# Attention scores of the second block on half-array tiles, and trailing means on VectorE

## The chip, the core and the metric

The kernel runs on one core of one Trainium2 chip. The metric is the device time of one execution in microseconds, as a median of several runs. A core has five engines that run in parallel, each with its own instruction queue: TensorE (PE in the profile), VectorE (DVE), ScalarE (ACT), GpSimd (POOL) and SyncE (SP), which here issues nearly all DMA transfers in the order of its queue.

## What is computed

The reference runs two transformer blocks over 256 tokens of width 1024. The first block (two layers: a linear-recurrent mixer and an attention, each with a feed-forward part) is not touched. In the second block the input is projected, and three things are computed side by side: a convolution with a layer norm, a sparse attention, and trailing means. They are joined, multiplied with an output matrix, added to the input, and a mixture of experts follows. What the change touches, cut:

```python
# sparse attention, a block of 128 queries at a time
rel = relu(einsum('bqhd,bsd->bqhs', qi_block, ki))        # indexer: 8 heads of 64, one key of 64
score = einsum('bqhs,bqh->bqs', rel, wi) * idx_scale      # then the 64 best keys of each query
q = einsum('btc,chd->bthd', cq, w_uq)                     # 8 heads of 64
# scores of the softmax over the chosen keys alone, then probabilities times values

# trailing means over windows of 2, 4, 8, 16 tokens, one for each of four groups of 64 channels
cs = cumsum(u); mean = (cs - cs shifted by w) / min(n_pos, w)
out = (mean - u) @ pool_w[g] * pool_scale
```

## The kernel before

All tensors stay on chip as float32; activations are held as features x tokens (128 partitions, 256 tokens), so a head of 64 features takes half of the 128 partitions, and two heads share a tile. Large products are made of three products of a high and a low part: `split_tile` (L115 loads, L122 rounds on ScalarE, L123 subtracts on VectorE, or on GpSimd when `eng` says so), `mm3` (L143 to L145).

The function `second` (L1171 on) is the second block up to the output product. It is written in program order; a planner orders each engine's instructions by that order as priority and by its own estimate of when inputs are ready, so that late steps fill gaps. `tc.issue_after` holds steps behind a named one. In program order:

- `proj(c0, use)` loads 256 columns of the input weights, splits them (on VectorE; for c0 = 1536 on GpSimd) and multiplies; `use` takes the result out of PSUM. Order: 1024 and 1280 (convolution), 0 (latent key, and `kib`, the indexer's key), 256 and 512 (the indexer's queries `qi`), 768 (query latent), 1536 (`pe`, the input of the trailing means).
- `index(j2)`, L1271, twice: for two pairs of heads j and two blocks b of queries one matmul over all 128 rows (L1277). Both heads' queries are the weights, and `kib` holds the key twice, block-diagonally, with zeros elsewhere (L1252, L1253 set them on GpSimd), so that head 0 and head 1 fall into different columns of the result. A Relu on ScalarE (L1279) and weighted sums on VectorE (L1283, L1285) follow.
- `kbd[j]`: the keys of a head pair, block-diagonal in the same way: two memsets on GpSimd (L1315, L1316), a matmul (L1318), two copies of 64 partitions on ScalarE (L1319, L1320). Then the values (L1323).
- eight rounds of top-8 on VectorE (L1332, L1334), and the mask (L1336).
- `soft(j)`, L1366, for four head pairs: scores (L1373), masked maximum on VectorE (L1377, L1378), exponentials on ScalarE (L1380), normalisation (L1382, L1385, L1387). `context(j, e)`, L1390: transposes (L1395), copies (L211, L213), values (L1400, L1401), split.
- `pool_mean`, L1408: eight steps on GpSimd (L1411 to L1418) behind two memsets; `pooled` multiplies (L1423).
- `convolved`, L1426: 46 steps on VectorE (L1434, L1436) and a layer norm with transposes (L1444, L1459); last in program order, so it fills gaps.
- `out2`, L272: the output product in four slabs of weights, of which the second half of the second slab is split on GpSimd; first slab from contexts 0 and 1, second from 2 and 3, third from the trailing means, fourth from the convolution.

The order at the end is written out: soft(0); then for j = 0 to 3: soft(j+1), context(j), the trailing means after j = 0, `pooled` after j = 1, the convolution after j = 3.

The expert weights of the mixture (196 pieces of up to 1 MB) are loaded by `fetch` (L1512, L1514) into buffers in turn: ten that are free early, then five in the pool `we`, which takes the place in memory of the second block's pools R2 and following (`kbd` was allocated first there, then `qi`, `sel`, `c2`, ... the convolution's `cv`), then buffers of the output weights and of the splits.

Of the kernel before, what the change touches and what calls it, by code (L numbers as in the profile page):

```python
# [9 lines left out]
F32 = mybir.dt.float32  # L10
# [9 lines left out]
S = 256  # L20
# [32 lines left out]
def tile_body(ctx, tc, a, out, stop=None, dbg=None):  # L53
# [17 lines left out]
    def psb():  # L71
        return ppool[0].tile([128, 512], F32, name="pb")
# [1098 lines left out]
    def second(R, diag, mcf, yT, raw, turned, last_square, ss2, consts):  # L1171
# [6 lines left out]
        def t2(name, slot):  # L1178
            return R2.tile([128, 2, 16 + S], F32, name=name, tag=f"t{slot}")
# [8 lines left out]
        nc.sync.dma_start(kvg, a["kv_g"].partition_broadcast(128))  # L1188
        kbd = [R2.tile([128, 2, S], F32, name=f"kbd{j}") for j in range(4)]
        qi = R2.tile([128, 4, S], F32, name="qi", tag="q")  # L1190
# [40 lines left out]
        def proj(c0, use, eng=None):  # L1231
            w = split_cols(a["w_z"][:, c0:c0 + 256], 256, eng)
            for i in range(2):
                p = psa()[:, 0:256]
                mm_feat3(p, w[i], hT, KT)
                use(i, p)
# [12 lines left out]

        kib = t2("kib", 1)[:, :, 0:S]  # L1250
        with tc.issue_after(after.ins):
            G.memset(kib[64:128, 0, :], 0.0)  # L1252
            G.memset(kib[0:64, 1, :], 0.0)  # L1253

        def use0(i, p):
            if i == 0:
                A.copy(ck, p)
            else:
                V.tensor_copy(kib[0:64, 0, :], p[0:64, :])
                A.copy(kib[64:128, 1, :], p[0:64, :])  # L1260
                A.activation(wf8[64:72, :], p[64:72, :], AF.Copy, scale=512.0 ** -0.5)
# [9 lines left out]
        def index(j2):  # L1271
            for j in (2 * j2, 2 * j2 + 1):
                for b in range(2):
                    nk, sc = 128 * (b + 1), sel[b]
                    p = psb()
                    p2 = p[:, 0:2 * nk].rearrange("p (h k) -> p h k", h=2)
                    T.matmul(p2, qi[:, j, b * 128:(b + 1) * 128], kib[:, :, 0:nk], start=True, stop=True)  # L1277
                    rel = RD.tile([128, 2, 256], F32, name="rel", tag="de", padded_shape=[128, 2, 384])
                    A.activation(rel[:, :, 0:nk], p2, AF.Relu)  # L1279
                    for i in range(2):  # L1280
                        w = wit[:, b, 2 * j + i:2 * j + i + 1]
                        if j + i == 0:
                            V.tensor_scalar(sc, rel[:, i, 0:nk], w, None, op0=mult)  # L1283
                        else:
                            V.scalar_tensor_tensor(sc, rel[:, i, 0:nk], w, sc, op0=mult, op1=add)  # L1285
        p = psb()
# [25 lines left out]
        for j in range(4):  # L1312
            t = kbd[j]
            with tc.issue_after(after.ins):
                G.memset(t[64:128, 0, :], 0.0)  # L1315
                G.memset(t[0:64, 1, :], 0.0)  # L1316
            p = psb()
            T.matmul(p[:, 0:256], w_uk[:, j * 128:(j + 1) * 128], ckT, start=True, stop=True)  # L1318
            A.copy(t[0:64, 0, :], p[0:64, 0:256])  # L1319
            A.copy(t[64:128, 1, :], p[64:128, 0:256])  # L1320
        for b in range(2):
# [40 lines left out]
        G.memset(pe[:, :, 0:16], 0.0)  # L1362
        proj(1536, lambda i, p: A.copy(pe[:, i, 16:], p), G)
        prefetch()

        def soft(j):  # L1366
            e = RD.tile([128, 2, 384], F32, name="de", tag="de")
            for b in range(2):
                nk = 128 * (b + 1)
                o = 0 if b == 0 else 128  # L1370
                p = psa()
                p2 = p[:, 0:2 * nk].rearrange("p (h k) -> p h k", h=2)
                T.matmul(p2, qT[:, j, b * 128:(b + 1) * 128], kbd[j][:, :, 0:nk], start=True, stop=True)  # L1373
                st = RW.tile([128, 8], F32, name="dst", bufs=4)
                eb = e[:, :, o:o + nk]
                for i in range(2):
                    V.tensor_tensor_reduce(eb[:, i, :], p2[:, i, :], sel[b], 1.0, -3e38, add, amax, st[:, i:i + 1])  # L1377
                V.tensor_scalar(st[:, 2:4], st[:, 0:2], rq[:, b:b + 1], -1.0, op0=mult, op1=mult)  # L1378
# [29 lines left out]
        def pool_mean():  # L1408
            G.memset(s2[:, :, 0:16], 0.0)
            G.memset(s4[:, :, 0:16], 0.0)  # L1410
            G.tensor_tensor(s2[:, :, 1:], pe[:, :, 1:], pe[:, :, 0:15 + S], add)  # L1411
            G.tensor_tensor(s4[:, :, 2:], s2[:, :, 2:], s2[:, :, 0:14 + S], add)
            G.tensor_tensor(s2[:, 1, 4:], s4[:, 1, 4:], s4[:, 1, 0:12 + S], add)
            G.tensor_copy(s2[64:128, 0, :], s4[64:128, 0, :])
            G.tensor_copy(s4[64:128, 1, :], s2[64:128, 1, :])
            G.tensor_tensor(s2[64:128, 1, 8:], s4[64:128, 1, 8:], s4[64:128, 1, 0:8 + S], add)
            G.tensor_tensor(pm, pm, pinv, mult)
            G.tensor_tensor(pm, pm, pe[:, :, 16:], sub)  # L1418

# [611 lines left out]
```

## Time and profile before

| | |
|---|---|
| median of 3 runs | 1334.0 us |
| the runs | 1334.43, 1330.85, 1334.0 us |
| profiled execution | 1335.32 us, span 1333.5 us |
| busy in the span: PE, DVE, ACT, POOL | 1166.8, 729.2, 491.3, 249.9 us |
| mean granted clock of TensorE | 0.936 |
| moved by DMA | 361.82 MB |

The span runs from the first to the last instruction of the profiled execution. Busy time is summed over all stages; what bounds one stage is read from tables by stretch and from timelines. A float32 matmul of the program appears as two records. A record "64*64" has 64 rows and 64 columns of the array. "idle" and the arrow behind a row say how long the engine had waited before it and which instruction ended the wait.

### The profile page before, as it was taken

The page shows a single profiled execution, that of the slowest core. Times are in us where ns is not written, and L with a number is a line of the kernel's source. Part 1 is how long each engine was busy: PE and PEld are TensorE (multiplying, and loading weights), DVE is VectorE, ACT ScalarE, POOL GpSimd, SP SyncE. Part 2 cuts the span into 40 slices and gives each one's busy share as a digit, 9 for nine tenths or more (in the row PEclk, how much of TensorE's full clock was granted, in tenths as well). Part 3 has the DMA queues.
Part 4 walks back from the last instruction along what each step waited for, and adds up shares of the span by engine and source line. Part 5 has one row for each costly group of instructions (what it writes and reads, how often), then busy time and mean ns, then how long its engine had stood idle before and what let it go on. Part 6 is the DMA issues. An engine that isn't in the chain of part 4 may idle for free.

```text
span 1333.5 us, 18894 instructions
## 1 busy us (share of the span) xinstructions
PE 1166.8 (87%) x7392; PEld 853.4 (64%) x7392; DVE 729.2 (55%) x1297; ACT 491.3 (37%) x857; POOL 249.9 (19%) x259
## 2 busy tenths in 40 slices
PE   7988899999999999999999999998877776666764
PEld 7987798988988888898999888662322131212211
DVE  6869947677687887657664789851112010101102
ACT  5624426454444656546444555620000000000002
POOL 5533330321211351122222233300000000000000
PEclk8999899999999999999999999999987677978788
DMA  7432206767775553667775853699999999999996
GB/s 243 132 90 92 80 33 218 264 237 284 279 289 190 173 186 127 219 234 248 255 243 179 332 193 138 245 357 420 418 420 418 420 417 419 420 417 421 418 421 262
DMA packets 129214, 361.82 MB, mean 271 GB/s; under 512 B 13408, under 2 KB 69344, under 8 KB 105568
## 3 DMA queue, kind: packets, MB, share of 16 engines
q1 hardware_dynamic: 126560, 359.24, 71.8%
q10 hardware_dynamic: 2560, 1.31, 0.4%
q8 instruction: 60, 0.98, 0.3%
q14 instruction: 34, 0.28, 0.1%
HBM read 358.96 MB, written 1.57 MB: 270 GB/s over the span
## 4 chain that ended last, share of the span: by engine, by line
PE 53%; DMA 28%; DVE 11%; issue 3%; ACT 3%; POOL 1%; SPq 0%; DVEq 0%; ACTq 0%; POOLq 0%
DMA ew<-in_exp_w_dram 15%; PE acc L144 9%; PE acc L143 9%; PE acc L145 9%; DMA ew<-in_exp_w2b_dram 8%; DMA wm<-in_mod_w_dram 4%; PE pb L143 3%; PE pb L145 3%; PE pb L144 3%; DVE s L123 3%; PE pb L1730 2%; PE pb L1704 2%; PE pb L1696 1%; PE pf L1704 1%; PE acc L1735 1%
## 5 line engine op out<-in xcount | busy, mean ns | idle before, releaser
L123 DVE TENSOR_TENSOR s<-w,s 128x1024 fp32r<-128x1024 f32 x224 | 285.2, 1276 | 93.1 <-ACT s L122 93.0
L122 ACT CAST s<-w 128x1024 fp32r<-128x1024 f32 x240 | 250.9, 1046 | 117.1 <-PE acc L145 88.7
L144 PE MATMUL pb<-xTh,s 128*128 128x256 f32 x512 | 144.3, 282 | 0.8 <-DVE s L123 0.8
L143 PE MATMUL pb<-xTh,s 128*128 128x256 f32 x512 | 144.5, 282 | 0.6 <-ACT xTh L153 0.6
L145 PE MATMUL pb<-xTl,s 128*128 128x256 f32 x512 | 144.1, 281 | 0.0
L942 POOL TENSOR_TENSOR ul<-u,uh 128x256 fp32r<-128x256 f32 x64 | 86.8, 1356 | 252.7 <-ACT uh L941 252.7
L144 PE MATMUL acc<-s,ul 128*128 128x512 f32 x256 | 100.5, 393 | 0.7 <-POOL ul L942 0.6
L143 PE MATMUL acc<-s,uh 128*128 128x512 f32 x256 | 100.1, 391 | 0.0
L145 PE MATMUL acc<-s,uh 128*128 128x512 f32 x256 | 99.7, 390 | 0.0
L143 PEld LDWEIGHTS pb<-xTh,s 128*128 128x128 f32 x512 | 96.1, 188 | 4.7 <-issue 1.7
L144 PEld LDWEIGHTS pb<-xTh,s 128*128 128x128 f32 x512 | 96.2, 188 | 4.0 <-DVE s L123 2.0
L145 PEld LDWEIGHTS pb<-xTl,s 128*128 128x128 f32 x512 | 98.0, 191 | 0.4 <-DVE xTl L154 0.4
L1709 DVE SCALAR_TENSOR_TENSOR big<-big,pb 128x512 f32<-128x512 f32 x8 | 5.5, 687 | 164.1 <-ACT big L1708 164.1
L143 PE MATMUL acc<-xTh,s 128*128 128x256 f32 x320 | 93.2, 293 | 2.2 <-ACT xTh L1225 1.5
L1704 PE MATMUL pb<-ew,big 128*32 128x512 f32 x448 | 68.8, 710 | 28.1 <-DMA ew<-in_exp_w_dram 24.0
L1730 PE MATMUL pb<-ew,big 128*32 128x512 f32 (+1 forms) x544 | 75.6, 672 | 19.8 <-DMA ew<-in_exp_w2b_dram 14.2
L1704 PE MATMUL pf<-ew,big 128*32 128x512 f32 x448 | 69.1, 724 | 27.3 <-DMA ew<-in_exp_w_dram 27.3
L144 PE MATMUL acc<-xTh,s 128*128 128x256 f32 x320 | 91.3, 286 | 0.0
L145 PE MATMUL acc<-xTl,s 128*128 128x256 f32 x320 | 90.6, 286 | 0.0
L1570 ACT ACTIVATE big<-pb,mc,gs 128x128 f32<-128x128 f32 x28 | 12.8, 458 | 192.8 <-DVE big L1572 192.8
L1763 POOL TENSOR_TENSOR frs<-frs,mhalf 128x1 f32<-128x1 f32 x2 | 1.1, 551 | 439.1 <-DVE frs L1761 439.1
L322 DVE SCALAR_TENSOR_TENSOR macc<-wm,cond,macc 128x512 f32<-128x512 f32 x84 | 65.8, 806 | 26.4 <-DMA wm<-in_mod_w_dram 26.2
(595 smaller groups left out, 2281.6 us busy)
## 6 DMA issues: line engine op xcount, KB each, us to landing
ew<-in_exp_w_dram SPq DMA_DIRECT2D x128, 1024.0 KB, 19.8
w<-in_w_up_dram SPq DMA_DIRECT2D x32, 1024.0 KB, 5.7
w<-in_w_down_dram SPq DMA_DIRECT2D x32, 1024.0 KB, 5.8
ew<-in_exp_w2a_dram SPq DMA_DIRECT2D x32, 1024.0 KB, 19.8
ew<-in_exp_w2b_dram SPq DMA_DIRECT2D x28, 1024.0 KB, 20.1
wm<-in_mod_w_dram SPq DMA_DIRECT2D x24, 1024.0 KB, 7.8
w<-in_w_in_ar_dram SPq DMA_DIRECT2D x14, 1024.0 KB, 5.5
w<-in_w_qkv_dram SPq DMA_DIRECT2D x12, 1024.0 KB, 5.1
```

The costliest lines, as they stand in the source:

```text
L122: A.copy(hi, src)
L123: (eng or V).tensor_tensor(lo, src, hi, sub)
L143: T.matmul(p, lhs[0], rhs[0], start=start, stop=False)
L144: T.matmul(p, lhs[1], rhs[0], start=False, stop=False)
L145: T.matmul(p, lhs[0], rhs[1], start=False, stop=stop)
L322: V.scalar_tensor_tensor(ac, wq, cond[:, k:k + 1], ac, op0=mult, op1=add)
L942: lows[:] = [G.tensor_tensor(ul, u, uh, sub)]
L1570: A.activation(dst, p, AF.Identity, scale=gs[:, kt:kt + 1], bias=sh[:, kt:kt + 1])
L1696: T.matmul(p[:, i * 128:(i + 1) * 128], x[:, tb, (k0 + i) * 128:(k0 + i + 1) * 128], oo[:, tb, :], start=(tb == 0), stop=(tb == 1))
L1704: T.matmul(p[32 * e:32 * e + 32, :], xg[:, k, 32 * e:32 * e + 32], t[:, e, :], start=(k == 0), stop=(k == KT - 1))
L1730: T.matmul(p[32 * e:32 * e + 32, :], ht[:, i, 32 * e:32 * e + 32], t[:, e], start=(i == 0), stop=(i == 3))
L1735: T.matmul(acc[tb][c // 512][:, c % 512:c % 512 + n], ogT[:, tb * 128:(tb + 1) * 128], y, start=first, stop=last, skip_group_check=True)
```

## The change

Three things. First, `kib` and `kbd[j]` hold keys of two heads on the two halves of the partitions, without the zeros: the ten memsets go, and `kbd[j]` is copied out of PSUM in one step. `index` and `soft` issue four matmuls for a head pair instead of two: for each block of queries b and each head h one matmul over 64 rows (partitions 0 to 63 or 64 to 127) into a PSUM bank for that head; both blocks of queries lie side by side in the bank (columns 0 to 127 and 128 to 383). So `index` makes one Relu a head over 384 columns instead of one a block. Second, the eight steps of `pool_mean` go from GpSimd to VectorE; the memsets stay. Third, the split of the weights of proj(1536) goes from GpSimd to VectorE.

```diff
-        kbd = [R2.tile([128, 2, S], F32, name=f"kbd{j}") for j in range(4)]
+        kbd = [R2.tile([128, S], F32, name=f"kbd{j}") for j in range(4)]
+        hp = (slice(0, 64), slice(64, 128))
+        span = (slice(0, 128), slice(128, 384))
...
-        kib = t2("kib", 1)[:, :, 0:S]
-        with tc.issue_after(after.ins):
-            G.memset(kib[64:128, 0, :], 0.0)
-            G.memset(kib[0:64, 1, :], 0.0)
+        kib = t2("kib", 1)[:, 0, 0:S]
...
-                V.tensor_copy(kib[0:64, 0, :], p[0:64, :])
-                A.copy(kib[64:128, 1, :], p[0:64, :])
+                V.tensor_copy(kib[0:64, :], p[0:64, :])
+                A.copy(kib[64:128, :], p[0:64, :])
...
             for j in (2 * j2, 2 * j2 + 1):
+                ps = psb(), psb()
                 for b in range(2):
-                    nk, sc = 128 * (b + 1), sel[b]
-                    p = psb()
-                    p2 = p[:, 0:2 * nk].rearrange("p (h k) -> p h k", h=2)
-                    T.matmul(p2, qi[:, j, b * 128:(b + 1) * 128], kib[:, :, 0:nk], start=True, stop=True)
-                    rel = RD.tile([128, 2, 256], F32, name="rel", tag="de", padded_shape=[128, 2, 384])
-                    A.activation(rel[:, :, 0:nk], p2, AF.Relu)
-                    for i in range(2):
-                        w = wit[:, b, 2 * j + i:2 * j + i + 1]
+                    for h in range(2):
+                        T.matmul(ps[h][:, span[b]], qi[hp[h], j, b * 128:(b + 1) * 128], kib[hp[h], 0:128 * (b + 1)],
+                                 start=True, stop=True)
+                rel = RD.tile([128, 2, 384], F32, name="rel", tag="de")
+                for h in range(2):
+                    A.activation(rel[:, h, :], ps[h][:, 0:384], AF.Relu)
+                for i in range(2):
+                    for b in range(2):
+                        sc, r, w = sel[b], rel[:, i, span[b]], wit[:, b, 2 * j + i:2 * j + i + 1]
...
         for j in range(4):
-            t = kbd[j]
-            with tc.issue_after(after.ins):
-                G.memset(t[64:128, 0, :], 0.0)
-                G.memset(t[0:64, 1, :], 0.0)
             p = psb()
             T.matmul(p[:, 0:256], w_uk[:, j * 128:(j + 1) * 128], ckT, start=True, stop=True)
-            A.copy(t[0:64, 0, :], p[0:64, 0:256])
-            A.copy(t[64:128, 1, :], p[64:128, 0:256])
+            A.copy(kbd[j], p[:, 0:256])
...
-        proj(1536, lambda i, p: A.copy(pe[:, i, 16:], p), G)
+        proj(1536, lambda i, p: A.copy(pe[:, i, 16:], p))
...
             e = RD.tile([128, 2, 384], F32, name="de", tag="de")
+            ps = psa(), psa()
+            for b in range(2):
+                for h in range(2):
+                    T.matmul(ps[h][:, span[b]], qT[hp[h], j, b * 128:(b + 1) * 128], kbd[j][hp[h], 0:128 * (b + 1)],
+                             start=True, stop=True)
             for b in range(2):
                 nk = 128 * (b + 1)
-                o = 0 if b == 0 else 128
-                p = psa()
-                p2 = p[:, 0:2 * nk].rearrange("p (h k) -> p h k", h=2)
-                T.matmul(p2, qT[:, j, b * 128:(b + 1) * 128], kbd[j][:, :, 0:nk], start=True, stop=True)
                 st = RW.tile([128, 8], F32, name="dst", bufs=4)
-                eb = e[:, :, o:o + nk]
+                eb = e[:, :, span[b]]
                 for i in range(2):
-                    V.tensor_tensor_reduce(eb[:, i, :], p2[:, i, :], sel[b], 1.0, -3e38, add, amax, st[:, i:i + 1])
+                    V.tensor_tensor_reduce(eb[:, i, :], ps[i][:, span[b]], sel[b], 1.0, -3e38, add, amax, st[:, i:i + 1])
...
-            G.tensor_tensor(s2[:, :, 1:], pe[:, :, 1:], pe[:, :, 0:15 + S], add)
+            V.tensor_tensor(s2[:, :, 1:], pe[:, :, 1:], pe[:, :, 0:15 + S], add)
...
-            G.tensor_tensor(pm, pm, pe[:, :, 16:], sub)
+            V.tensor_tensor(pm, pm, pe[:, :, 16:], sub)
```

## Rows read from the trace of the kernel before

**Rows 1.** Page, the span in 40 equal slices: DMA busy tenths, GB/s

```profile
DMA  7432206767775553667775853699999999999996
GB/s 243 132 90 92 80 33 218 264 237 284 279 289 190 173 186 127 219 234 248 255 243 179 332 193 138 245 357 420 418 420 418 420 417 419 420 417 421 418 421 262
```

**Rows 2.** Busy time by stretch: us, busy of each engine (instructions), PEclk, DMA share, GB/s

```profile
780.00:838.00 58.00, 58.00 (x401) 52.16 (x400) 51.97 (x135) 28.58 (x58) 16.86 (x24) 1.00 0.42 146
838.00:852.00 14.00, 11.27 (x49) 6.21 (x48) 13.24 (x53) 10.53 (x33) 9.54 (x9) 1.00 0.77 300
852.00:886.00 34.00, 33.98 (x179) 26.51 (x177) 20.26 (x45) 16.23 (x42) 1.81 (x4) 1.00 0.75 287
...
860.00:900.00 40.00, 37.32 (x215) 27.61 (x217) 24.53 (x84) 13.58 (x31) 1.12 (x2) 1.00 0.90 344
...
900.00:1000.00 100.00, 79.85 (x596) 28.09 (x588) 16.04 (x42) 7.49 (x16) 0.00 (x0) 0.95 1.01 419
```

**Rows 3.** Chain that ended last, in order of time, 815 to 851: start us, us, what

```profile
818.86 1.94 PE pb L1323 x4
820.79 2.58 PE pb L1277 x8
```

**Rows 4.** Timeline of PE: start us, us, engine, line, operation, shape, records

```profile
147.57 0.41 PE L682 MATMUL pb<-Tu,El 64*64 64x32 f32 x4
...
151.75 0.89 PE L682 MATMUL pb<-Tu,El 64*64 64x32 f32 x24
...
838.04 3.17 PE L1373 MATMUL acc<-kbd,qT 128*128 128x256 f32 x10
...
847.81 0.38 PE L1401 MATMUL pb<-deT,vv 128*64 128x128 f32 x2
848.12 0.66 PE L1395 MATMUL pb<-ident,de 128*128 128x128 f32 x4
```

**Rows 5.** Groups by line and shape, 700 to 960: busy us, mean ns, idle before

```profile
L123 DVE TENSOR_TENSOR s<-w,s 128x1024 fp32r<-128x1024 f32 x40 | 49.5, 1243 | 21.8 <-ACT s L122 21.8
...
L1279 ACT ACTIVATE rel<-pb 128x512 f32<-128x512 f32 x4 | 2.4, 603 | 3.1 <-DVE sc L1285 2.3 <-PE pb L1277 0.8
...
L1499 DVE TENSOR_TENSOR x<-x,mix 128x512 f32<-128x512 f32 x3 | 2.1, 688 | 0.1
...
L211 ACT COPY deT<-pb 128x384 f32<-128x384 f32 x4 | 1.9, 475 | 2.2 <-PE pb L1395 2.2
...
L1320 ACT COPY kbd<-pb 64x256 f32<-64x256 f32 x4 | 1.5, 368 | 0.0
```

**Rows 6.** Who waited for the instructions that write or read kbd: us, times

```profile
  PEld pb L1323: 0.7, 2
```

**Rows 7.** Timeline of POOL, 775 to 900

```profile
814.50 8.01 POOL L123 TENSOR_TENSOR s<-w,s 128x1024 fp32r<-128x1024 f32 x2 [3.34 <-ACT s L122]
...
840.91 2.35 POOL L123 TENSOR_TENSOR s<-w,s 128x1024 fp32r<-128x1024 f32 x1
...
847.34 1.27 POOL L1418 TENSOR_TENSOR s<-s,pe 128x512 f32<-128x512 f32 x1
```

**Rows 8.** Timeline of DVE, 775 to 900

```profile
801.63 4.43 DVE L1436 SCALAR_TENSOR_TENSOR cv<-late,ckh,cv 128x256 f32<-128x256 f32 x11
...
814.95 5.36 DVE L1436 SCALAR_TENSOR_TENSOR cv<-late,ckh,cv 128x256 f32<-128x256 f32 x8
821.74 3.03 DVE L1285 SCALAR_TENSOR_TENSOR sc<-rel,wit,sc 128x128 f32<-128x128 f32 x7 [1.43 <-ACT rel L1279]
...
841.08 2.19 DVE L1378 TENSOR_SCALAR dst<-dst,rq 128x2 f32<-128x2 f32 x1
...
847.93 1.23 DVE L1387 TENSOR_TENSOR de<-de,dst 128x512 f32<-128x512 f32 x1
```

**Rows 9.** Waits of the DMA queue, 843 to 872: us in total, times, longest

```profile
SPq L1514 <- PE pf L1459: 8.0, 1, 8.0
SPq L1514 <- DVE dst L1377: 5.9, 1, 5.9
```

## What the change does to the time: a prediction

> **What bounds the kernel now.** I read four views in this order. The page's slices come first: from the 28th slice on the DMA engines are busy in nine tenths or more, at about 420 GB/s, to the end [rows 1]. That is the stream of expert weights; at 900 to 1000 us it moves 419 GB/s with a DMA share of 1.01 [rows 2]. So the end is set by when that stream gets going without gaps, and the second block before it (780 to 886 us) decides that: its last part hands over the buffers that the loads wait for. Between 860 and 900 us the mean is only 344 GB/s [rows 2], so 40 x (1 - 344/419) = 7.2 us of stream time are lost there to buffers that come late. A microsecond that the second block saves is a microsecond off the end, as long as the loads' buffers follow.
>
> Next the table by stretch [rows 2]. The reader is to see three stages. From 780 to 838 us TensorE is busy in 58.00 of 58 us: the projections and the indexer are bound by TensorE, at full granted clock. From 838 to 852 us (the softmax scores) it is busy in 11.27 of 14 us while VectorE has 13.24 and ScalarE 10.53: the chain through VectorE and ScalarE is the bound, TensorE waits. From 852 to 886 us TensorE has 33.98 of 34 us (contexts and output product). So a matmul shortened in the first stage counts, one in the second hardly does, and what counts there is when the first contexts reach the output product.
>
> Then the chain and the timelines, for the price of single steps [rows 3, 4, 7, 8], and last the waits of the DMA queue [rows 9].
>
> **The change part by part.** The sum goes against the profiled execution: span 1333.5 us, 1335.3 us as timed, against a median of 1334.0. I take the difference from 1334.0.
>
> *Indexer scores.* Half the indexer is one run of 8 records, 2.58 us on the chain [rows 3]; both halves 5.2 us. The changed form sends the same columns, each half as many rows deep, and the two heads use different halves of the array. Whether halves run side by side is seen in the first block: four 64-row records there take 0.41 us, the first to last start some 0.06 us each, and twenty-four with alternating row halves take 0.89 us, some 0.03 us each [rows 4]. I read that as two at a time, so the indexer's TensorE time falls by 2.6 us. The shapes differ (there also the columns differ, here all 128 columns are used by both halves), so the bounds are 0 and 2.6 us. What the switch of shape costs: the indexer's 3072 columns in 2.58 us are 0.84 ns a column [rows 3], so two 128-column records are worth 0.22 us; from such a pair on 64 array columns at 847.81 to the full-array record at 848.12 it is 0.31 us [rows 4], so some 0.09 us a switch. Three or four blocks of indexer matmuls, in and out, make 0.6 us. Net gain 2.0 us, between -0.6 and 2.6.
>
> The rule that speaks against this stands in the Trainium skill, TensorEngine Tiling (Array Packing), section Key Properties: a change of tiling mode drains TensorE. The row just named agrees in kind. By the rule alone without the concurrency that the same page promises, the indexer would lose the 0.6 us instead of gaining 2.0, and the sum below would be about 0.4 us.
>
> *Copies of the keys.* Eight copies of 64x256 (0.368 us each [rows 5]) become four of 128x256; a copy's time goes by columns (256 columns 0.37, 384 columns 0.475, 512 columns 0.60 [rows 5]), so ScalarE saves 4 x 0.37 = 1.5 us, right before the last half of the indexer. TensorE waited 0.7 us for these copies at the value matmuls [rows 6]. I take 0.7 us; bounds 0 and 1.5. The indexer's two Relu of 384 columns (2 x 0.475) replace one of 256 and one of 512 (0.37 + 0.60): nothing. The removed memsets lie on an idle GpSimd long before use: nothing, and if that cover were gone they would only help.
>
> *Two weight splits to VectorE.* proj(1536) took GpSimd 8.01 us [rows 7], VectorE needs 2 x 1.24 = 2.5 us [rows 5]. But the pair cost VectorE time already: eight convolution steps beside it took 5.36 us, while eleven took 4.43 us elsewhere, so 8 x 0.40 = 3.2 and 2.1 us were stall [rows 8]. Net +0.4 us, hidden: VectorE sat idle 1.43 us just before the top-k chain [rows 8], and convolution steps, last in priority, can move back. Queued behind the splits on VectorE are those convolution steps, and behind them the top-k; bounds 0 to +2.5. The output weights' second slab, whose buffer the splits release, comes earlier; nothing waits for it.
>
> *Softmax scores.* The ten records at 838.04 run 3.17 us back to back [rows 4]; they halve, but TensorE idles 2.7 us in that stage, so only the first head pair's latency is shorter: 0.3 us. Both heads' scores must now be ready for both row blocks before a PSUM bank is freed; four banks serve two head pairs, as before. Bounds 0 and 1.5.
>
> *Trailing means.* Eight GpSimd operations go to VectorE. By 0.688 us for 512 columns of two inputs [rows 5], with 542, 540, 268, 264, twice 512 columns and two half copies of 272: 0.73 + 0.73 + 0.36 + 0.36 + 1.38 + 2 x 0.36 = 4.3 us, in the stage where VectorE has 13.24 of 14 us. Against it: the normalisation at 847.93 took 1.23 us beside a GpSimd operation that ended at 848.61, its own 512 columns are worth 0.69; 0.5 us come back [rows 5, 7, 8]. The large stall stays: the two-column step at 841.08 took 2.19 us, to 843.27, and GpSimd's operation beside it (840.91 to 843.26) is the output weights' split, which the change leaves [rows 7, 8]. On GpSimd's queue only that split stood behind the means; it can go sooner. The means stand behind soft(1) and context(0) in priority, before soft(2); so the first contexts are not late, the later ones may be. From 852 on TensorE has the output product's first slab to work on meanwhile. I take 0, between +3.8 (all in front of soft(2)) and -2.2 (the stall no longer falls on the chain).
>
> Sum: 2.0 + 0.7 + 0.3 = 3.0 us. The forecast is 1334.0 - 3.0 = 1331.0 us; with the bounds of the indexer and copies, 1329 to 1333.
>
> *The buffers.* The four key tiles shrink from 8 to 4 KB a partition at the bottom of a pool, whose place five 8 KB load buffers take over later. The second of these now also covers the convolution's tile. So its load, which before went after the last masked score (a wait of 5.9 us on L1377), must wait for the convolution's last transposes (L1459, 8.0 us of wait for the next load) [rows 9]. One megabyte, 1.05 MB at 419 GB/s = 2.5 us, moves behind that point, into the 7.2 us lost there. It costs nothing unless L1459 ends more than 7.2 - 2.5 = 4.7 us later than now; it caps the gain at 4.7 us if L1459 doesn't move.
>
> **The rivals.**
>
> *One half after the other.* The array's halves take turns, the indexer loses 0.6 us; 0.7 + 0.3 - 0.6 = 0.4 us remain: 1333.6. For: no row has both halves on all columns. Against: the pairs of the first block.
>
> *VectorE takes the gain back.* The means and the splits land before soft(2) and soft(3), TensorE runs out of output product and waits: 3.0 - 3.8 + some of the 0.3: about 1334.5. For: 13.24 of 14 us. Against: VectorE's stalls that leave, and 13.7 us free from 852 to 886 [rows 2].
>
> *The convolution's tail blocks the DMA queue.* 4.3 us of means, 2.5 us of splits and a 2.2 us stall push the last-priority convolution back by 9.0 us. Past 4.7 us the queue's head waits for L1459 and the stream starts later: +4.3, 1338.3. For: the head of the queue waits there already, 8.0 us [rows 9]. Against: the stage before gets shorter, which pulls the tail forward.
>
> *More is freed.* The 2.19 us stall falls on a mean instead of on the chain, the 0.5 us come back too: 5.7 us less, 1328.3, if the tail moves forward with it. The Trainium skill, SBUF — State Buffer, section Who interferes with whom, has the rule: a VectorE instruction with two SBUF inputs, or in a two-port mode, and a GpSimd one that reads SBUF exclude each other for a whole instruction. The large stall ends with GpSimd's operation to 0.01 us, so it bears the rule out.
>
> **How the numbers follow.** Forecast 0.44; more freed 0.21; VectorE 0.16; one after the other 0.09; the tail 0.10. A measurement of this kernel can tell about 0.3%, 4 us: faster means under 1330.0. That takes 0.20 of the freed case and 0.11 of the forecast's spread: 0.31. The tail gives slower 0.09. The rest, 0.60, is no change. The range leaves out the tail and the far end of the freed case: 1327.0 to 1337.0.
>
> **What would show it.** Right: two 64-row records with starts closer than one's stream time, half of the indexer near 1.4 us instead of 2.58; the last score before the softmax 2 to 3 us earlier; expert loads from 900 us on as dense as now but that much earlier. Wrong: records spaced as before; TensorE idle between 852 and 880; a wait on L1459 that ends after 865.

## The result, and the profile after

The changed kernel takes 1349.1 us (median of 4 runs, 1347.5 to 1352.6) beside 1334.2 us for the kernel before (median of 4, 1330.9 to 1339.1): a ratio of 1.0106, 95% interval 1.0081 to 1.0131. It is slower by 11 to 17 us, and lies outside the predicted range. The profiled execution has a span of 1346.7 us, 1348.4 us as timed.

The table by stretch, same columns and stretches as [rows 2], of the kernel after:

```profile
780.00:838.00 58.00, 57.13 (x422) 52.03 (x421) 54.08 (x145) 28.94 (x59) 8.18 (x14) 1.00 0.46 158
838.00:852.00 14.00, 11.06 (x70) 7.76 (x68) 12.93 (x42) 8.53 (x26) 2.35 (x1) 0.88 0.63 248
852.00:886.00 34.00, 32.75 (x157) 24.30 (x157) 21.53 (x57) 16.93 (x43) 0.90 (x2) 1.00 0.33 123
860.00:900.00 40.00, 39.04 (x202) 29.19 (x202) 27.09 (x90) 14.61 (x34) 1.44 (x3) 0.96 0.64 253
900.00:1000.00 100.00, 79.57 (x579) 28.21 (x577) 16.87 (x44) 8.40 (x18) 0.00 (x0) 0.94 1.02 419
```

Two things stand out. Between 852 and 886 us the DMA engines moved 123 GB/s where they had moved 287, and from 900 us on they are as dense as before. And in the softmax stretch TensorE's granted clock is 0.88 where it was 1.00.

The first is seen in the DMA queue's own timeline (start us, us to the last issue, line, transfer, count). It was not among the rows of before, so here is the kernel before first:

```profile
838.65 5.00 SPq L115 DMA_DIRECT2D w<-in_w_out_dram  x2
845.57 22.00 SPq L1514 DMA_DIRECT2D ew<-in_exp_w_dram  x6
872.66 6.17 SPq L1514 DMA_DIRECT2D ew<-in_exp_w2a_dram  x4
882.86 4.29 SPq L1512 DMA_DIRECT2D ew<-in_exp_w2b_dram  x4
```

and the same stretch of the kernel after, with one line of its queue's waits from 843 to 880 us:

```profile
840.59 3.69 SPq L115 DMA_DIRECT2D w<-in_w_out_dram  x2
868.42 0.34 SPq L1513 DMA_DIRECT2D ew<-in_exp_w_dram  x1
876.27 6.17 SPq L1513 DMA_DIRECT2D ew<-in_exp_w2a_dram  x4
882.79 5.47 SPq L1513 DMA_DIRECT2D ew<-in_exp_w_dram  x5
888.35 6.05 SPq L1511 DMA_DIRECT2D ew<-in_exp_w2b_dram  x4
```

```profile
SPq L1513 <- DVE s L123: 28.3, 2, 20.9
```

Before, six expert loads went out from 845.57 us on. After, one of the six stands at the head, waits 20.9 us for VectorE's split of an output weight slab (its target is a slab buffer), and the other five come behind the four w2a loads, at 882.79 us. The order in which the queue issues is fixed when the kernel is built, by a planner that weighs when it thinks each buffer comes free. This kernel's planner had chosen another order. So the first load goes out 22.9 us later than the first one of before, and the next not until 876.27 us. What that costs is read from one stretch, before and then after (columns as in [rows 2]):

```profile
846.00:876.00 30.00, 28.95 (x140) 21.28 (x141) 18.84 (x51) 16.37 (x44) 3.44 (x4) 1.00 0.67 256
846.00:876.00 30.00, 27.64 (x132) 19.20 (x129) 21.81 (x64) 18.92 (x52) 0.90 (x2) 0.95 0.21 80
```

30 us at 176 GB/s less are 5.3 MB, or 12.6 us of the stream at 419 GB/s, beside the 13.2 us by which the span grew (the later start of 4.0 us, below, is part of both). Behind that the stream is bound by its rate to the end: from the last residual (L1498) to the end it is 458.8 us where it was 449.2.

For the bookkeeping the profiled execution is cut at two points: the start of the second block (its reciprocal norms are copied, L1220, before L1216) and the last residual. Start: 777.9 us against 773.9. Block: 110.0 against 110.4. Tail: 458.8 against 449.2. The instructions ahead of the start are the same in every kernel here, and the start lies anywhere from 769.8 to 778.5 in the 20 profiles of this study, so the first 4.0 us are chance. The block, which was to lose 3.0 us, lost 0.4.

### The profile page after: what moved, and what is told of

The parts are those of the page before. It is cut to its first block, busy times and chain, and to the rows that moved or that the text cites. A ratio compares the mean times of both kernels' runs of the same rounds, so it can differ in the third digit from the quotient of the medians.

```text
span 1346.7 us, 18927 instructions
## 1 busy us (share of the span) xinstructions
PE 1175.0 (87%) x7424; PEld 854.2 (63%) x7424; DVE 730.4 (54%) x1307; ACT 490.0 (36%) x853; POOL 231.5 (17%) x239
## 3 DMA queue, kind: packets, MB, share of 16 engines
q10 hardware_dynamic: 2560, 1.31, 0.4%
HBM read 358.96 MB, written 1.57 MB: 268 GB/s over the span
## 4 chain that ended last, share of the span: by engine, by line
PE 50%; DMA 28%; DVE 9%; issue 7%; POOL 3%; ACT 3%; SPq 0%; ACTq 0%; DVEq 0%; POOLq 0%
DMA ew<-in_exp_w_dram 18%; DMA ew<-in_exp_w2b_dram 9%; PE acc L144 9%; PE acc L145 9%; PE acc L143 9%; PE pb L143 3%; PE pb L145 3%; PE pb L144 3%; DVE s L123 2%; POOL ul L942 2%; PE pb L1729 1%; PE pb L1703 1%; PE pf L1703 1%; PE acc L862 1%; PE pb L1695 1%
## 5 line engine op out<-in xcount | busy, mean ns | idle before, releaser
L123 DVE TENSOR_TENSOR s<-w,s 128x1024 fp32r<-128x1024 f32 x226 | 288.2, 1278 | 93.4 <-ACT s L122 92.8
L1703 PE MATMUL pf<-ew,big 128*32 128x512 f32 x448 | 72.2, 745 | 30.6 <-DMA ew<-in_exp_w_dram 30.6
L1703 PE MATMUL pb<-ew,big 128*32 128x512 f32 x448 | 73.3, 752 | 25.2 <-DMA ew<-in_exp_w_dram 21.6
L1762 POOL TENSOR_TENSOR frs<-frs,mhalf 128x1 f32<-128x1 f32 x2 | 1.1, 548 | 448.9 <-DVE frs L1760 448.9
```

Of the source, the lines that this page charges most:

```text
L123: (eng or V).tensor_tensor(lo, src, hi, sub)
L1703: T.matmul(p[32 * e:32 * e + 32, :], xg[:, k, 32 * e:32 * e + 32], t[:, e, :], start=(k == 0), stop=(k == KT - 1))
```

## Experiments

All runs at a glance. Medians beside those of the kernel before on the same chip; "block", "softmax" (first score, from its weight load, to last residual) and "tail" in us from the profiled execution; "clock" is the lowest granted clock of the 5 us slices from the first score to the last context; "loads" is the issue of the first expert load behind the output weights. In e16 to e18 "softmax" holds a projection that stood ahead of it in the others.

| run | this / before, us | ratio, 95% interval | block | softmax | tail | clock | loads |
|---|---|---|---|---|---|---|---|
| before | | | 110.4 | 46.4 | 449.2 | 1.00 | 845.6 |
| after | 1349.1 / 1334.2 | 1.0081 to 1.0131 | 110.0 | 47.9 | 458.8 | 0.66 | 868.4 |
| e1 old key places | 1346.8 / 1336.5 | 1.0045 to 1.0101 | 115.0 | 52.0 | 454.6 | 0.50 | 873.1 |
| e2 before, half the keys | 1345.8 / 1336.5 | 1.0057 to 1.0117 | 110.2 | 47.1 | 461.0 | 1.00 | 869.3 |
| e3 rows only | 1340.5 / 1336.5 | 1.0029 to 1.0074 | 113.1 | 50.4 | 448.7 | 0.50 | 842.2 |
| e4 before, means and splits on VectorE | 1340.7 / 1336.5 | 1.0026 to 1.0068 | 112.0 | 47.8 | 455.2 | 1.00 | 868.6 |
| e5 index rows only | 1336.6 / 1336.4 | 0.9978 to 1.0024 | 109.9 | 47.2 | 448.9 | 1.00 | 844.4 |
| e6 softmax rows only | 1338.9 / 1336.4 | 1.0000 to 1.0038 | 111.9 | 48.6 | 448.9 | 0.74 | 849.1 |
| e7 softmax rows twice | 1341.3 / 1336.4 | 1.0030 to 1.0070 | 115.4 | 52.3 | 449.2 | 0.54 | 853.0 |
| e8 after, old load order | 1353.3 / 1336.4 | 1.0095 to 1.0159 | 112.5 | 49.2 | 463.7 | 0.50 | 848.0 |
| e9 rows, long fill | 1342.1 / 1333.9 | 1.0038 to 1.0079 | 117.5 | 54.3 | 451.1 | 0.57 | 852.7 |
| e10 before, splits on VectorE | 1334.2 / 1333.9 | 0.9983 to 1.0016 | 109.9 | 46.3 | 448.9 | 1.00 | 843.4 |
| e11 before, means on VectorE, old order | 1335.9 / 1333.9 | 0.9996 to 1.0031 | 110.1 | 47.8 | 449.7 | 1.00 | 844.2 |
| e12 index rows, splits on VectorE | 1335.2 / 1333.9 | 0.9984 to 1.0019 | 109.6 | 46.3 | 449.1 | 1.00 | 846.3 |
| e13 before, half scores | 1335.1 / 1335.5 | 0.9987 to 1.0029 | 110.9 | 48.1 | 449.2 | 0.50 | 841.3 |
| e14 rows, short fill | 1347.1 / 1335.5 | 1.0070 to 1.0126 | 115.3 | 52.5 | 450.4 | 0.57 | 857.8 |
| e15 after, no load turn | 1340.5 / 1335.5 | 1.0029 to 1.0058 | 112.2 | 48.4 | 450.6 | 0.50 | 848.7 |
| e16 rows, scores ahead | 1337.7 / 1336.7 | 0.9990 to 1.0030 | 109.6 | 52.0 | 449.2 | 0.67 | 843.9 |
| e17 before, scores ahead | 1333.7 / 1336.7 | 0.9964 to 0.9998 | 108.3 | 50.9 | 447.7 | 1.00 | 850.5 |
| e18 index rows, scores ahead | 1334.8 / 1336.7 | 0.9969 to 1.0004 | 108.6 | 49.9 | 449.0 | 1.00 | 847.9 |

### What turned the loads

**e1**, the changed kernel with its buffers where they were:

```diff
-kbd = [R2.tile([128, S], F32, name=f"kbd{j}") for j in range(4)]
+kbd = [R2.tile([128, 2, S], F32, name=f"kbd{j}")[:, 0, :] for j in range(4)]
```

> The changed kernel, with each key tile kept at its old 2 KB a partition (only its first half is used), so every later buffer lies where it lay before the change. Theory P (places): the freed 4 KB shifted the buffers behind it, one expert load came to lie on the buffer of a late VectorE split, and with it five 1 MB loads went behind the w2a loads; with the old size the queue has six loads, four w2a, four w2b again, the DMA engines are busy between 850 and 876 us as before, and the time falls by 9 us, to 1340 (1336 if the 4 us by which the second block began later were chance). Theory V (VectorE): the loads are late because VectorE's queue got the splits and the trailing means; then nothing changes, 1349.

**e2**, the reverse, on the kernel before:

```diff
-kbd = [R2.tile([128, 2, S], F32, name=f"kbd{j}") for j in range(4)]
+kbd = [R2.tile([128, 2, S], F32, name=f"kbd{j}") for j in range(2)] * 2
```

> The kernel before, with two key tiles instead of four (the third and fourth head pairs overwrite the first two, so half of the keys' products are left out of the output, while every instruction stays): 4 KB fewer, all engines' work as before. Theory P: the queue turns as in the changed kernel, six loads become one, four w2a, five, and the time rises by 9 us, to 1343. Theory V: no change, 1334.

**e4**, the kernel before with `proj(1536, ...)` without its argument `G` and the eight operations of `pool_mean` on `V`:

> The kernel before with the two splits of the pooling columns and the trailing means moved to VectorE, nothing else. Theory P: the score maxima wait behind some 7 us of means in pieces, the softmax ends 1 to 2 us later, 1335 to 1336. Theory V: 1343 to 1349, with the five loads late.

Neither theory held alone; both causes are there, and each is enough. The waits of the DMA queue from 843 to 880 us in e1, e2 and e4, one line each:

```profile
SPq L1513 <- DVE s L123: 24.8, 1, 24.8
```

```profile
SPq L1514 <- DVE s L123: 27.4, 2, 22.4
```

```profile
SPq L1514 <- DVE s L123: 28.2, 2, 24.4
```

In e2 every instruction stays and only 4 KB of place goes, and the queue has the order of the kernel after (one, four w2a, five): theory P, tail 461.0. In e4 no place changed, and in e1 the old places are restored, but with the means on VectorE the planner puts the slab buffer's load ahead of the other five all the same; they then go out together, from 868.6 (e4) and 873.1 us (e1), ahead of w2a. The tail is 455 us in both. e1 missed its 1340 us because the second cause was still in it.

**e10** has the splits alone on VectorE; **e11** the means alone, with each load of the first group held behind the one before it:

```diff
-return ahead.pop(0) if ahead else fetch(slot, src)
+if ahead:
+    return ahead.pop(0)
+with tc.issue_after(loads[-1].ins) if turn[0] < 25 else nullcontext():
+    return fetch(slot, src)
```

> The kernel before with the two splits of the pooling columns on VectorE, the means still on GpSimd; the expert loads keep their order. If the splits are what the run with both moves (1340.7) lost: 1339 or more. If the means alone turned the load order and delayed the softmax: 1335 to 1336.5, at most 1 us from the kernel before.

> The kernel before with the trailing means alone on VectorE and the expert loads held to the order of before. If the means cost through the load order (the load on the slab buffer at the head, waiting for a VectorE split until 868 us): the loads start by 846 us, 1335 to 1337. If they cost through the later softmax: 1339 to 1341, with the last context 3 us or more later than in the kernel before, counted from the first score.

The splits cost nothing that can be told (1.0000, interval -0.17% to 0.16%), and with them the loads start at 843.4 us as before. With the old order the means cost nothing that can be told (interval -0.04% to 0.31%), although the last context comes 29.9 us after the first score instead of 25.2: the output product has other work meanwhile. So the means cost through the queue. The means alone with the planner's own order were not run; e4 and e10 together put the turn on them.

**e8** puts the same edit on the changed kernel:

> The changed kernel as it is, small key tiles and means on VectorE, with each expert load of the first group held behind the load before it, which gives the queue the order of the kernel before (five into the pool that opens after the block, then the one into the slab buffer, then w2a). If the order of the queue alone costs the 9 us: loads start by 846 to 850 us, 1349 falls to 1340. If the buffers are truly taken longer in the new places: the first five issue only after 865 us all the same, and 1345 or more stays.

It is the slowest of all. The queue's waits, 843 to 892 us:

```profile
SPq L1513 <- DVE ct L1453: 17.4, 1, 17.4
SPq L1513 <- DVE x L1498: 16.4, 1, 16.4
```

In order again, the loads run into buffers that are truly taken: the second waits for the convolution's tile, and the fifth for the last residual (issued at 891.1 us). With the smaller key tiles the planner's turned order was, by the medians, the lesser evil (the intervals of the two kernels overlap); among the runs here only those with the old places (e3, e15) are free of this half of the loss.

**e15** takes both causes out (old key size, means on GpSimd, splits left on VectorE):

> The changed kernel with the old key size and the means back on GpSimd, the splits left on VectorE: the change without the two parts that turned the order of the expert loads. The loads start by 850 us as before; what is left of the 13 to 15 us is the lower clock of the softmax: 1336 to 1340. If the turn of the loads were not what cost most: 1344 or more.

1340.5 us, +0.43%. So the turned loads, with whatever the means cost on VectorE besides, were some 8 to 10 of the 14 to 15 us, and 5 to 6 are left.

### What the row groups do

**e3** is e15 with the splits on GpSimd as well. **e5** is the kernel before with the changed `use0` and `index` alone, **e6** with the changed `soft` and key copies alone in tiles of the old size.

> The changed kernel with the old size of the key tiles and with the two splits and the trailing means back on GpSimd: only the row groups are left. Theory P: the gain of the indexer's scores with nothing against it, 1331 to 1333 (before less 1 to 3). Theory V with the splits and means as cause: the same, 1331 to 1333, but then the run with the old key size alone must be far slower than this one, 1349. If the row groups themselves cost: 1336 or more.

> The kernel before with the row groups in the indexer alone; the softmax scores, the key tiles, the splits and the means stay. Theory C (clock): the three kernels whose softmax scores take row groups had the granted clock at 0.50 for 7 to 16 us in the softmax stage, the others 1.00; with the softmax as before the clock stays 1.00 there, the indexer gives back 1.3 to 2 us, 1334 to 1335 beside 1336 for the kernel before. Rival (the row groups of the indexer lower the clock too, or their gain is taken back): 1336 or more.

> The kernel before with the row groups in the softmax scores alone, key tiles in their old places, expert loads in the old order. Theory C: the clock falls to 0.50 somewhere between the first score and the last context, the stage from the first score to the last residual takes 49 to 52 us (46.4 before), the time rises by 2 to 5 us, 1338 to 1341. Rival (the clock's dips in that stage were chance): clock 1.00, stage 45 to 46.5, time 1335 to 1336.

The indexer alone gives nothing that can be told (e5), the softmax alone loses at most 0.38% (e6, at the edge of its interval), both together lose 0.29% to 0.74% (e3). Why both lose more than the one and the other (0.51% beside 0.01% and 0.19%) stays open; e3's profiled execution is the fastest of its twelve and shows less of the loss than the median. Half an indexer run of TensorE in the kernel after, timeline as in [rows 4]:

```profile
809.62 0.93 PE L1277 MATMUL pb<-kib,qi 64*128 64x128 f32 x8
810.48 0.39 PE L143 MATMUL acc<-xTh,s 128*128 128x256 f32 x1
810.70 0.28 PE L144 MATMUL acc<-xTh,s 128*128 128x256 f32 x1
...
811.79 1.30 PE L1277 MATMUL pb<-kib,qi 64*128 64x128 f32 x8 [0.24 <-ACT rel L1281]
```

The same place in the kernel before:

```profile
807.00 1.45 PE L1277 MATMUL pb<-kib,qi 128*128 128x256 f32 x4
807.90 0.68 PE L143 MATMUL acc<-xTh,s 128*128 128x256 f32 x1
808.41 0.28 PE L144 MATMUL acc<-xTh,s 128*128 128x256 f32 x1
```

In the first head pair the two heads do run side by side: the records' starts come in twos, no more than 0.01 us apart. From its first record to the second full-array record behind it, it is 810.70 - 809.62 = 1.08 us, where the kernel before had 808.41 - 807.00 = 1.41 us: 0.33 us saved, where the prediction had 0.65 without the cost of the switches and 0.5 with it. The second pair waits 0.24 us for the Relu of the first, since a pair now holds two PSUM banks until both Relus are done. Its second head gets its bank 0.38 us after the first, and the records start singly, not in twos: 1.45 us where it was 1.57. The last two pairs take 2.63 us together where they took 2.70, with a wait of 0.33 us inside. These waits, 0.6 us over the indexer, are new.

In the softmax the clock falls. Stretches of 2 us of the kernel before (columns as in [rows 2]):

```profile
841.00:843.00 2.00, 1.41 (x4) 0.37 (x3) 2.00 (x2) 0.69 (x2) 2.00 (x1) 1.00 0.97 403
843.00:845.00 2.00, 1.23 (x4) 0.65 (x5) 2.00 (x15) 1.69 (x7) 1.86 (x5) 1.00 1.03 418
845.00:847.00 2.00, 1.39 (x8) 0.62 (x6) 1.86 (x6) 1.90 (x8) 1.92 (x2) 1.00 1.01 399
```

and after:

```profile
841.00:843.00 2.00, 1.60 (x15) 1.00 (x12) 2.00 (x10) 0.45 (x1) 1.47 (x1) 1.00 0.89 315
843.00:845.00 2.00, 0.57 (x4) 0.17 (x3) 2.00 (x10) 1.06 (x5) 0.87 (x1) 1.00 0.93 383
845.00:847.00 2.00, 2.00 (x9) 1.17 (x10) 1.89 (x8) 2.00 (x7) 0.00 (x0) 0.59 1.03 406
847.00:849.00 2.00, 1.62 (x7) 1.21 (x7) 1.53 (x7) 2.00 (x9) 0.00 (x0) 0.55 1.02 399
```

VectorE is as busy as ever, TensorE stands still, and its granted clock goes from 2.4 to 1.2 GHz (0.59 and 0.55 are means over 2 us) just when the transposes and contexts begin. What the scores stand still for is VectorE: a head pair now holds two of the four PSUM banks until the maxima of both row blocks are taken, where a bank was free after the maxima of its one block. Timeline of PE, two lines of the kernel before, then two of the kernel after:

```profile
843.62 0.67 PE L1373 MATMUL acc<-kbd,qT 128*128 128x256 f32 x2 [0.77 <-DVE dst L1377]
844.44 1.10 PE L1373 MATMUL acc<-kbd,qT 128*128 128x512 f32 x2 [0.15 <-DVE dst L1377]
841.93 1.48 PE L1369 MATMUL acc<-kbd,qT 64*128 64x128 f32 x8 [0.33 <-DVE dst L1376]
844.84 2.10 PE L1369 MATMUL acc<-kbd,qT 64*128 64x128 f32 x8 [1.43 <-DVE dst L1376]
```

With the means on GpSimd this wait is longer, in e6 (waits of PE, 838 to 866 us):

```profile
PE acc L1369 <- DVE dst L1376: 3.7, 3, 3.2
```

There two two-column steps of VectorE (L1377) ahead of that maximum took 3.40 us beside GpSimd's operations. In e3, e6 and e15 the last score ends 8.2 to 9.7 us after the first starts, later than before (7.5); in the kernel after, e1 and e8 it ends sooner (6.2 to 6.9). So the row groups in the softmax bring two things, these waits and the lower clock; in the six kernels with row groups there and no added or moved work (after, e1, e3, e6, e8, e15) the two come together, and no run prices the waits by themselves.

The dip is in every kernel whose softmax scores take row groups, 10 of 10: 3.4 us of it in the kernel after, 13.7 in e1, 10.2 in e3 (not the 7 to 16 us of e5's expectation). The stage took 47.9 us in the kernel after, as long as with the means on VectorE and no dip (47.8 in e4 and e11), and 48.4 to 54.3 in the other nine, of which e7, e9 and e14 carry more matmuls and e16 the projection.

Is it the idling, or the row groups themselves? **e7** issued each softmax matmul twice, **e9** and **e14** put multiplications by the identity behind the second pair's scores (`T.matmul(p, ident, vv[:, 0, :], ...)`, nine and four times), **e13** let the full array compute half as much (the maxima of both heads read the first head's scores). Row kernels here are built on e3; in e7, e9, e13, e14 and e16 to e18 the loads are held in order as in e11.

```diff
-T.matmul(p2, qT[:, j, b * 128:(b + 1) * 128], kbd[j][:, :, 0:nk], start=True, stop=True)
+T.matmul(p2[:, 0, :], qT[:, j, b * 128:(b + 1) * 128], kbd[j][:, 0, 0:nk], start=True, stop=True)
```

> Row groups in indexer and softmax, old key places, means and splits on GpSimd, each matmul of the softmax scores issued twice into the same place, and the expert loads held to the order of before. Theory C: TensorE is as busy in the softmax as before the change, the clock stays 1.00 and the stage takes 46 to 47.5 us, the time 1334 to 1336, although there is more work than in the run with the rows once (1340). Rival (the rows once lost their time otherwise): 1340 to 1342, the clock whatever it is.

> Row groups in indexer and softmax, old key places, means and splits on GpSimd (as in the run with the rows only, 1340.5), and nine 128x512 multiplications by the identity, whose result nobody reads, behind the scores of the second head pair, where TensorE idled before its clock fell (0.18 to 0.95 us busy of 2 us); the issuing twice of the scores had left that gap open. Theory G (the gap lowers the clock): no stretch below 1.00 between 835 and 870 us, first score to last residual 46.5 to 48 us (50.4 without), time 1336 to 1338. Rival (row groups lower the clock by themselves): clock at 0.50 for some us all the same, 50 us or more, 1340 or more.

> The kernel before, where each softmax score instruction computes one head of the two over all 128 rows of the array (the second head's scores are left out, the first's are used twice): as few score columns as with row groups, but none of them in row groups. Theory G (TensorE's idle time in the softmax lowers the clock): 0.50 for some us between 838 and 862, as in the seven kernels with row groups there; first score to last residual 48 us or more, 1337 to 1340. Rival R (the row groups themselves lower it): clock 1.00 throughout, stage 45.5 to 47.5 us, 1333 to 1335.

> The kernel with row groups and the idle time behind the second pair's scores filled, with four multiplications in place of nine, since nine took 7.5 us where the gap has 3 to 4. [...] Rival R: 0.50 for some us whatever is filled, 50 us or more, 1339 or more.

In e7, e9 and e14 the clock fell all the same: each only moved the idle time. The nine multiplications took 8.0 us, and behind them the first context still waited 1.8 us for VectorE; behind the four, TensorE was busy 0.04 us of 845 to 847 and 0.47 of 847 to 849, and the clock fell there. e13 tells whether row groups are needed. None of its scores take them; stretches of 2 us:

```profile
839.00:841.00 2.00, 0.74 (x3) 0.42 (x3) 2.00 (x5) 1.59 (x6) 1.94 (x3) 1.00 0.98 397
841.00:843.00 2.00, 0.28 (x2) 0.00 (x0) 2.00 (x10) 0.98 (x4) 1.84 (x4) 1.00 0.99 360
843.00:845.00 2.00, 1.27 (x4) 0.68 (x5) 1.68 (x10) 1.87 (x7) 1.92 (x2) 0.55 1.08 440
845.00:847.00 2.00, 2.00 (x10) 1.45 (x8) 1.34 (x7) 0.59 (x3) 1.79 (x3) 0.50 0.93 395
```

So row groups are not needed for the dip. What all eleven dips have in common is idle time of TensorE, 1.31 us (e16) to 3.94 us (e7) in one piece, shortly ahead of the fall or around it. That it is the cause is argued from this, and idle time alone doesn't decide: e11 and e17 had pieces of 1.47 and 1.54 us there and kept 1.00. The dip's price in e13 was below what I expected: the stage took 48.1 us instead of 46.4, with 6.8 us at 1.2 GHz, and the median moved by nothing that can be told. That the clock is all of the 5 us left in e15 is not shown. Its 6.8 us at half the clock can hold 3.4 us of lost work at most (an estimate, 6.8 x 0.5), and its last scores waited 2.8 us for VectorE's maxima. In e15's profile the block is longer by 1.8 us and the tail by 1.4, and how the rest comes about stays open.

**e12** joins the two parts that turn nothing, rows in the indexer and splits on VectorE:

> The kernel before with row groups in the indexer alone and the two splits on VectorE: the two parts of the change that turn neither the load order nor the clock. Gain of the indexer 0.6 us as in the run with its rows alone, of the splits 0 to 1.5: 1334 to 1336, at best 0.1% under the kernel before. Rival (the splits cost VectorE time ahead of the score maxima): 1337 or more.

Their sum is nothing that can be told, either.

### Work for the idle time

The projection of the pooling columns (48 matmuls, some 0.118 us from start to start, 5.7 us) stood ahead of the scores. Moved behind the first pair's scores it can run while the first softmax does, with row groups (**e16**), in the kernel before (**e17**) and with e12 (**e18**), the loads held in order as in e11:

```diff
-proj(1536, ...)
-prefetch()
...
 e = soft(0)
+proj(1536, ...)
+prefetch()
```

> Row groups in indexer and softmax, old key places, means and splits on GpSimd, expert loads held to the old order, and the scores of the first head pair put ahead of the projection of the pooling columns, so that TensorE has 5.6 us of projection to do while VectorE and ScalarE work on the first softmax. Theory G: the idle time goes, the clock stays at 1.00, the two ends together (second block's start to last residual) come under 110 us (113.1 with the rows and no move), 1331 to 1334. Rival (the gap opens later all the same, behind the other pairs): clock 0.50 for some us, 113 us, 1338 or more.

> The kernel before with only that move of the first pair's scores, and the expert loads held to the old order. TensorE idled some 2.7 us of the ten behind its scores, at full clock: theory G gives 0.5 to 2 us back, 1333 to 1335; the rival that the projection, whose result the means on GpSimd wait for, then ends later and with it the last output columns, 1336 or more.

> Row groups in the indexer alone, splits on VectorE, the first pair's scores ahead of the projection, loads in the old order. If the move is worth its gap, 1332 to 1334; if the gap opens later all the same, 1335 to 1337 as without it.

With row groups it gives the block 3.5 us back (109.6 against e3's 113.1) and makes the kernel level with the one before, but the gap opens again between 835 and 839 us and the clock falls to 0.50 for some 3 us. Best of all is the move alone: e17, 0.19% faster than the kernel before (interval 0.02% to 0.36%, barely clear of noise for the best of eighteen runs), 1.2% faster than the changed one by the two ratios. e18 is the same within its interval.

## Why the prediction was wrong

*What bounds the kernel* held: the stream of expert weights sets the end, at 419 GB/s, and the second block decides when it gets going.

*The buffers* is the step that failed, and with it the answer. It said of the load that moves behind the convolution's end: "It costs nothing unless L1459 ends more than 7.2 - 2.5 = 4.7 us later than now". The place was right (e8: the second load waits for the convolution's tile), but two things were missed. A shift of 4 KB moves every buffer above it, and the fifth load came to lie on one that the last residual frees. And I treated the queue's order as given, when the planner makes it anew from its estimates: the front-most load changed from one that was ready at 845 us to one that was ready at 868. e2 measures this step by itself at 0.57% to 1.17%, where I had nothing.

*Trailing means.* The cost on VectorE agrees with the bounds: e11 adds -0.5 to 4.1 us with the queue in order, and the prediction's value 0 is in it. That the means could turn the queue stood nowhere among the rivals; the rival of the convolution's tail came nearest (the queue's head waits, 1338.3) and had the wrong instruction: the wait was on a weight split (L123), not on L1459. e4, with the splits moved as well, shows +0.26% to 0.68%.

*Indexer scores*: -2.0 us predicted, and the whole stage from the first index matmul to the first softmax score went from 31.0 to 30.4 us in e5. The two-at-a-time reading of the first block's rows was right for the pair that finds both its banks free; the size was wrong. In the kernel after, the four pairs save 0.33, 0.12 and, the last two together, 0.07 us instead of 0.5 each, with 0.6 us of new waits on the Relus, which I had set at nothing because their columns add up the same: a bank is now held until a pair's work is done. The Trainium skill, TensorEngine Tiling (Array Packing), section Gotcha 1: PSUM Pressure, says that different row tiles write to different PSUM banks, so that the pressure on the banks grows; the 0.6 us of new waits agree. The same page of the Trainium skill, section Key Properties, says that a change of tiling mode drains TensorE; what that took in the first pair, no row here separates.

*Copies of the keys*: -0.7 predicted. With e6 the part up to the last key copy is shorter by 1.4 us (11.86 against 13.29, from the first index matmul on), and the part behind it, to the first score, longer by 1.1 us; 0.3 us remain. The 0.7 us of [rows 6] are a wait of PEld, the weight loads; TensorE's matmuls were never out of work there before ([rows 2], 58.00 of 58 us), so a copy that was waited for only changed the order of its work.

*Softmax scores*: a gain of 0.3 with bounds 0 and 1.5 predicted, a loss in fact: e6 0.00% to 0.38% slower. "four banks serve two head pairs, as before" put no price on a bank that is held for both row blocks: the scores waited 0.9 us for VectorE's maxima before, 1.8 us in the kernel after and 3.7 us in e6. "TensorE idles 2.7 us in that stage" was read as cover; in all ten kernels with row groups there the clock fell behind the idle time, and in this stage of the kernel before it never did, so its rows gave no price for it. That a shorter matmul may cost was not among the bounds. How the loss divides between the waits and the clock stays open.

*Two splits*: 0, and nothing that can be told measured (e10).

*More is freed*: the large stall stayed and changed place. The same two-column steps took 1.68 us from 842.35 on (L1377, two of them), to 844.03, beside GpSimd's split from 841.53 to 843.88.

*The range*: the sum's own bounds reach 1334.3 us (1334.0 + 0.6 - 0.3, with the indexer and the copies at their worst), not 1333; the measured time lies outside either.

## What to carry to other kernels

A change of a buffer's size is a change of every buffer behind it and, where a planner orders the queues, of the order of the transfers: compare the queue's order before and after, ahead of any sum over instructions. Price a moved operation twice, once on its engine and once for what it does to the buffers that transfers wait for. And before a matmul is shortened beside a chain on other engines, ask what frees the banks that it writes to and what TensorE will do in the time won; if the answer to the second is nothing, give it work first (e17 won more by moving a projection than the row groups did by halving the scores).

## What the runs showed of the hardware

Row groups of 64 start in pairs 0.01 us apart where both PSUM banks are free, yet such a head pair's index scores, up to the second full-array record behind them, became only 23% shorter (1.41 to 1.08 us); where the second bank came 0.38 us later, 8% (1.57 to 1.45 us).

TensorE's granted clock fell to 0.50 after stretches in which it idled for 1.3 to 3.9 us in one piece, with 0.57 busy of 2 us (after) or 0.28 of 2 us (e13) right before, and stayed down for 3.4 to 13.7 us in this stage. A stretch alone doesn't tell: in e17 TensorE was busy 0.46 us of 844 to 846, between two stretches full of work, and kept 1.00:

```profile
842.00:844.00 2.00, 2.00 (x12) 1.32 (x10) 2.00 (x4) 2.00 (x6) 0.00 (x0) 1.00 0.52 74
844.00:846.00 2.00, 0.46 (x5) 0.32 (x4) 1.74 (x8) 1.84 (x5) 1.02 (x1) 1.00 0.69 274
846.00:848.00 2.00, 2.00 (x9) 1.10 (x8) 2.00 (x11) 1.33 (x5) 1.92 (x3) 1.00 0.93 387
```
